# Decoder block on one core: gates of the last two attention-output jobs loaded a row block sooner, sums of the gated weights in place, another written order

## The chip, the cores and the metric

The kernel runs on one core of one Trainium2 chip. Each engine takes its instructions in order: PE (TensorE matmul, with its weight load PEld), DVE (VectorE), ACT (ScalarE), POOL (GpSimd) and SP (SyncE), which here only issues DMAs. Engines wait for each other and for DMAs through semaphores. The metric is the device time of one execution in microseconds (us); lower is better. The time before is 2249.14 us, the median of 3 runs (2249.02 to 2251.96).

## The reference

One block with a recurrent and an attention branch. What matters here is its end:

```python
y_rnn = (hr * silu(z_rnn)) @ w_out_rnn
y_attn = (o * silu(z_attn)) @ w_out_attn
merged = sigmoid(g_r + bg_r) * y_rnn + sigmoid(g_a + bg_a) * y_attn
x = x + gate[:, None, :] * (merged @ w_o)
return rms_norm(x, g_final)
```

The sequence has 2048 positions, the model 1024 channels. All is float32.

## The kernel before

**Splitting.** A float32 matmul is made of three on rounded operands: a value is split into a high part (rounded by ACT, `hi_act`, L158) and a low part (value less high, by DVE, `lo_dve` L167, or by POOL, `lo_pool` L164). `mm3` (L152) then adds high times high, high times low and low times high. All matmuls are therefore recorded at L150.

**Output jobs.** `steps` (L1657) computes both branch outputs, transposed, in eight jobs: four column blocks of 512 positions for the recurrent branch, then four for attention. A job has eight row blocks of 128 channels, so there are 64 row blocks, numbered 0 to 63 here (`t` in the code). A row block is eight steps k, each one `mm3` of a 128 x 128 weight and a y tile of 128 x 512. The first six jobs (blocks 0 to 47) are spread between the units of attention; the last two (blocks 48 to 63, columns 1024 to 2047) run on their own, 128 steps one after another, with only the work of the next stage beside them. The change is in these.

**Weights.** The weights of a row block come in two pieces of four steps, so 128 pieces in all; piece x lies in tile S0 to S3, by x % 4. `load_w` issues piece x + 3 in the second step of piece x on SP's queue, and SP waits there until PE has done with the tile. From piece 98 on the weight comes raw (L1673, from `wR`, 256 KB) and is split on the core: `split_w`, high on ACT, low on DVE, recorded at L158 and L167 as S<-S.

**Gates.** The sum of a row block (pj in PSUM) is multiplied by the attention gate and the gated recurrent output is added: `load_g` loads the two gate tiles fg (L1712, from `gaT` and `mrT`) in step 3 of the block, `evict` (L1717 the product, L1719 the add, both DVE) runs in step 1 of the next block, and `store` (L1724, SP) writes the block to `meT` in step 7 of the next. The four fg buffers hold two row blocks; which buffer a tile gets is the tile framework's choice, and a load waits for the last reader or for the store of what lay in it.

**The y tiles.** The eight y tiles of the next job are loaded (L346, four buffers R) and split while the last rows of a job run; in this stage ACT makes the highs, POOL the lows of even k and DVE those of odd k.

**Rows of the next stage.** Beside these steps `w_o` is made ready for the last stage, a seven-product scheme on 2 x 2 blocks (`product`, `output_pair`). For each of four row pairs k, `load_rows` loads two rows blocks of `w_o` (128 x 1024 each, st1/st2 or st3/st4), `gate_rows` multiplies them by the residual gate (L1849, POOL), `difference` makes four sums T1 to T4 (L1861, DVE), and `high` and `low` split the three blocks and four sums that the scheme needs. `build_rows` gives each of these a step: 10, 34, 74 and 98 for the four row pairs, and an offset. An offset fixes only the place in each engine's order; an engine does an instruction as soon as it is at its head and its operands are there. All these tables are written by hand.

**Queues.** SP's order mixes weight pieces, gates, stores and y tiles, and a load that waits for its buffer holds all behind it. A DMA on SP also waits for the one eight issues earlier.

After block 63 the stage of `output_pair` starts (lines 1958 to 2056), with PE at work without waits worth naming until about 2225 us.

Of the kernel before, what the change touches and what calls it, by code (L numbers as in the profile page):

```python
# [10 lines left out]
F32 = mybir.dt.float32  # L11
# [4 lines left out]
ALU = mybir.AluOpType  # L16
# [4 lines left out]
P = 128  # L21
S = 2048
D = 1024
KT = D // P
NB = 4
# [64 lines left out]
def decoder_block(ctx, tc, x, c, positions, g_norm, w_mod, b_mod, w_in, b_gate, conv_w, conv_b,  # L90
# [4 lines left out]
    def T(pool, shape, dt, tag, **kw):  # L95
        cnt[0] += 1
        return pool.tile(shape, dt, tag=tag, name=f"{tag}_{cnt[0]}", **kw)
# [68 lines left out]
    def lo_dve(o, i, h):  # L166
        return nc.vector.tensor_tensor(o, i, h.bitcast(F32), ALU.subtract).ins  # L167
# [1483 lines left out]
            at(e + 2, TAIL, self.store)  # L1651

    stored = set()
    RAW = 2 * KT * (NB + 2) + 1


    def steps(jobs):  # L1657
# [17 lines left out]
        def split_w(x):  # L1675
            if RAW < x < 2 * len(tiles):
                raw = W[x][:, 1].bitcast(F32)
                hi_act(W[x][:, 0], raw)
                lo_dve(W[x][:, 1], raw, W[x][:, 0])

        def load_y(j, k):
            if j < len(jobs):
# [22 lines left out]
        def load_g(t):  # L1705
            j, m = tiles[t]
            w, ys, n = jobs[j]
            at_ = slice(m * P, (m + 1) * P), slice(n * CH, (n + 1) * CH)
            G[t] = []
            for src in (grT,) if ys is yaT else (gaT, mrT):  # L1710
                g = T(fl, [P, CH], F32, "fg", bufs=4)
                nc.sync.dma_start(g[:], src[at_])  # L1712
                G[t].append(g)

# [6 lines left out]
        def store(t):  # L1721
            j, m = tiles[t]
            w, ys, n = jobs[j]
            nc.sync.dma_start((mrT if ys is yaT else meT)[m * P : (m + 1) * P, n * CH : (n + 1) * CH], G.pop(t)[0][:])  # L1724

        for k in range(KT):
            split_y(0, k)
        yield
        last = None
        for t, (j, m) in enumerate(tiles):  # L1730
            ps = T(pj, [P, CH], F32, "pj")
            for k in range(KT):
# [4 lines left out]
                    load_w(2 * t + k // KH + 3)  # L1737
                if k == 1 and t:
                    evict(t - 1, last)
                if k == 3:  # L1740
                    load_g(t)
                if k == 7 and t:
                    store(t - 1)
                wt = W[2 * t + k // KH]
                yh, yl = Y[j, k]
                mm3(ps[:], wt[:, 0, k % KH, :], wt[:, 1, k % KH, :], yh[:], yl[:], first=k == 0, last=k == KT - 1)
# [86 lines left out]
    def on(n, fn, *args):  # L1833
        pend.setdefault(n, []).append((fn, args))
# [14 lines left out]
        nc.gpsimd.tensor_tensor(v[k, i][:], v[k, i][:], v["gate"][:], ALU.mult)  # L1849

    def part(name, k):
        name = {"T3": "B12", "T4": "B21"}.get(name, name)
        if name[0] == "T":
            if (name, k) not in v:
                v[name, k] = T(fp, [P, KH, P], F32, {"T1": "s1", "T2": "s2"}[name])
            return v[name, k][:].rearrange("p k j -> p (k j)")
        i, j = int(name[1]) - 1, int(name[2]) - 1
        return v[k, i][:, j * CH : (j + 1) * CH]

    def difference(name, k, a, b):  # L1860
        tt(part(name, k), part(a, k), part(b, k), ALU.subtract)  # L1861

    def high(name, k):
        hi_act(B[name][0][:, k, :], part(name, k))
# [2 lines left out]
        lo(B[name][1][:, k, :], part(name, k), B[name][0][:, k, :])  # L1867

    def build_rows(s, k):
        on(s, gate_rows, k, 0)  # L1870
        on(s + 5, gate_rows, k, 1)
        on(s + 6, high, "B11", k)
        on(s + 7, difference, "T1", k, "B12", "B11")
        on(s + 8, low, "B11", k, lo_dve)
        on(s + 11, high, "B21", k)
        on(s + 11, difference, "T2", k, "B22", "T1")
        on(s + 12, high, "B22", k)
        on(s + 12, difference, "T3", k, "B22", "B12")
        on(s + 13, high, "T1", k)
        on(s + 13, low, "B21", k, lo_dve)  # L1880
        on(s + 15, difference, "T4", k, "B21", "T2")
        on(s + 14, low, "B22", k, lo_pool)
        on(s + 15, high, "T2", k)
        on(s + 16, high, "T3", k)
        on(s + 16, low, "T2", k, lo_dve)
        on(s + 17, high, "T4", k)
        on(s + 17, low, "T1", k, lo_pool)
        on(s + 18, low, "T4", k, lo_dve)
        on(s + 19, low, "T3", k, lo_pool)

    A, ops = {}, {}
    NP = 2 * NB
# [237 lines left out]
```

## Time and profile before

| | before |
|---|---|
| median of 3 runs | 2249.14 us |
| profiled execution, its time | 2252.27 us |
| its span, first to last instruction | 2250.5 us |
| mean granted TensorE clock | 0.985 |
| start of block 48, end of block 63 (from the order of the records) | about 1965.1 and 2087.3 us |
| PE busy and mean granted clock between these | 103.25 of 122.20 us, 0.89 |
| DVE, ACT, POOL busy between these | 94.11, 40.14, 48.75 us |

The profiled execution is one execution under the hardware profiler; its span is 1.8 us shorter than its time. In a list of instructions a row gives start, duration, engine, line, operation, out<-in, count, and in brackets how long the engine stood idle before it and what released it. PE's busy time counts modelled ends of pipelined matmuls, so a busy PE is not PE at its peak. The granted clock is a share of full speed.

### The profile page before, as it was taken

What the parts mean: (1) busy time and instruction counts of PE and PEld (TensorE: products, weight loads), DVE (VectorE), ACT (ScalarE), POOL (GpSimd) and SP (SyncE); (2) the same over time, 40 slices, a digit from 0 to 9 for tenths busy, and PEclk for the clock granted to TensorE, in tenths of its full rate; (3) what the DMA queues carried; (4) which work ended last, traced back from release to release, by engine and by line L of the source; (5) the groups of instructions that cost most, each with busy time, mean ns of one, the idle gap of its engine ahead of it and who ended that gap; (6) DMA issues with size and microseconds to landing.
All of it is one profiled execution on the core that took longest, in us unless ns stands there. A gap on an engine that the chain in (4) does not pass through costs nothing.

```text
span 2250.5 us, 34124 instructions
## 1 busy us (share of the span) xinstructions
PE 2183.3 (97%) x11326; PEld 1843.5 (82%) x11326; DVE 1442.4 (64%) x2482; ACT 1282.9 (57%) x2554; POOL 1060.3 (47%) x784
## 2 busy tenths in 40 slices
PE   8999999999999999999999999999999998988998
PEld 5998888888778988888888877888888887866786
DVE  5839887878455715445445442666667776578887
ACT  6638678767534527556456203676778877533333
POOL 2557777667556322222222102555556655334443
PEclk9999999999999999999999999999999999998999
DMA  8467887887998368888989989888988887877543
GB/s 284 117 210 262 280 301 269 295 280 261 334 282 276 111 227 277 274 299 287 299 298 304 358 285 286 272 267 255 276 263 257 250 240 227 259 248 232 180 164 113
DMA packets 412133, 577.34 MB, mean 257 GB/s; under 512 B 72406, under 2 KB 270258, under 8 KB 410932
## 3 DMA queue, kind: packets, MB, share of 16 engines
q1 hardware_dynamic: 369748, 446.75, 63.4%
q10 hardware_dynamic: 42016, 128.36, 14.9%
q8 instruction: 90, 1.47, 0.3%
q14 instruction: 87, 0.71, 0.1%
q0 software_dynamic: 192, 0.05, 0.0%
HBM read 356.92 MB, written 218.11 MB: 256 GB/s over the span
## 4 chain that ended last, share of the span: by engine, by line
PE 52%; DMA 7%; DVE 4%; issue 4%; ACT 3%; POOL 3%; SPq 1%; ACTq 0%; POOLq 0%; DVEq 0%
PE X L150 10%; PE pj L150 10%; PE V L150 9%; PE W L150 5%; PE Z L150 5%; PE Y L150 4%; PE sc L150 4%; PE o L150 3%; DMA R<-in_w_in_dram 1%; PE pg L150 1%; PE pT L1505 1%; PE pT L1518 1%; DMA vraw<-vN 1%; DMA kraw<-qT 1%; DMA kraw<-kT 1%
## 5 line engine op out<-in xcount | busy, mean ns | idle before, releaser
L150 PE MATMUL pj<-yh,S 128*128 128x512 f32 x1024 | 376.4, 413 | 21.7 <-ACT S L158 9.0
L164 POOL TENSOR_TENSOR S<-R,S 128x512 fp32r<-128x512 f32 x168 | 255.6, 1529 | 173.6 <-ACT S L158 63.8
L150 PE MATMUL V<-T,S 128*128 128x512 f32 x1344 | 326.2, 392 | 4.8 <-DVE t L454 4.6
L150 PE MATMUL X<-T,S 128*128 128x512 f32 x1344 | 324.0, 390 | 1.4 <-POOL S L164 1.0
L150 PEld LDWEIGHTS V<-T,S 128*128 128x128 f32 x1344 | 252.9, 189 | 60.0 <-DVE t L454 3.0
L150 PEld LDWEIGHTS X<-T,S 128*128 128x128 f32 x1344 | 251.5, 188 | 55.5 <-POOL S L164 1.5
L150 PEld LDWEIGHTS pj<-yh,S 128*128 128x128 f32 x1024 | 197.9, 194 | 65.7 <-ACT S L158 11.5
L150 PE MATMUL pj<-yl,S 128*128 128x512 f32 x512 | 206.9, 404 | 10.3 <-POOL yl L164 5.6
L164 POOL TENSOR_TENSOR S<-s,S 128x512 fp32r<-128x512 f32 x92 | 140.2, 1524 | 116.3 <-ACT S L158 68.3
L1421 ACT ACTIVATE pp<-pp,st 128x256 f32<-128x256 f32 (+3 forms) x256 | 133.8, 524 | 96.5 <-DVE st L1420 95.4
L150 PE MATMUL Z<-T,S 128*128 128x512 f32 x672 | 161.9, 390 | 0.0
L150 PE MATMUL Y<-T,S 128*128 128x512 f32 x672 | 161.8, 390 | 0.0
L150 PE MATMUL W<-T,S 128*128 128x512 f32 x672 | 161.7, 389 | 0.0
L150 PEld LDWEIGHTS W<-T,S 128*128 128x128 f32 x672 | 126.0, 188 | 27.0 <-issue 0.9
L150 PEld LDWEIGHTS Y<-T,S 128*128 128x128 f32 x672 | 125.9, 188 | 26.0
L150 PEld LDWEIGHTS Z<-T,S 128*128 128x128 f32 x672 | 125.8, 188 | 26.1
L167 DVE TENSOR_TENSOR ptl<-pT,pth 128x384 fp32r<-128x384 f32 (+1 forms) x160 | 97.9, 629 | 75.8 <-ACT pth L158 73.6
L164 POOL TENSOR_TENSOR s<-R,s 128x512 fp32r<-128x512 f32 x32 | 45.4, 1418 | 201.6 <-ACT s L158 178.5
L912 DVE SCALAR_TENSOR_TENSOR xc<-xr,par,xc 128x512 f32<-128x512 f32 x96 | 98.9, 1030 | 47.3 <-ACT xc L906 45.0
L158 ACT ACTIVATE S<-R 128x512 fp32r<-128x512 f32 x168 | 101.5, 622 | 47.9 <-DMA R<-in_w_in_dram 23.1
L150 PEld LDWEIGHTS pj<-yl,S 128*128 128x128 f32 x512 | 99.7, 195 | 29.4 <-POOL yl L164 7.7
L1485 ACT ACTIVATE pp<-pp,M 128x256 f32<-128x256 f32 (+3 forms) x256 | 117.9, 522 | 9.9 <-DVE M L1608 9.9
(400 smaller groups left out, 4868.8 us busy)
## 6 DMA issues: line engine op xcount, KB each, us to landing
sD<-S ACTq DMA_DIRECT2D x196, 512.0 KB, 4.1
S<-sD SPq DMA_DIRECT2D x196, 512.0 KB, 5.0
S<-wD SPq DMA_DIRECT2D x98, 512.0 KB, 5.3
R<-in_w_in_dram SPq DMA_DIRECT2D x136, 256.0 KB, 4.3
wD<-s ACTq DMA_DIRECT2D x64, 256.0 KB, 5.2
T<-in_w_mod_dram SPq DMA_DIRECT2D x8, 1024.0 KB, 11.7
vN<-ev SPq DMA_DIRECT2D x64, 128.0 KB, 2.7
zaT<-ev SPq DMA_DIRECT2D x32, 256.0 KB, 4.4
```

The source lines that it names most:

```text
L150: nc.tensor.matmul(o, lhsT=l, rhs=r, start=st, stop=sp, **kw)
L158: nc.scalar.activation(o, i, AF.Copy)
L164: nc.gpsimd.tensor_tensor(o, i, h.bitcast(F32), ALU.subtract)
L167: return nc.vector.tensor_tensor(o, i, h.bitcast(F32), ALU.subtract).ins
L912: nc.vector.scalar_tensor_tensor(xc, xr[:, i : i + CH], cw(i), xc, ALU.mult, ALU.add)
L1421: nc.scalar.activation(pdst, pdst, AF.Exp, bias=m_, scale=-1.0, accum_out=l_)
L1485: nc.scalar.activation(pp, pp, AF.Copy, scale=w)
L1505: nc.tensor.transpose(pt[:, c0 + j * P : c0 + (j + 1) * P], pp[i][:, k * P : (k + 1) * P], ident)
L1518: nc.tensor.transpose(pt[:, c * P : (c + 1) * P], pp[:, half * P : (half + 1) * P], ident)
```

## The change

In the last two jobs (`t >= TAIL0`, 48):

- the gates of a block are loaded in step 3 of the block before (block 48 in its own step 0; blocks 62 and 63 in step 0 of themselves), and every third block (2, 5, 8, 11 of the stage) takes the tiles s1 and s2 of the next stage instead of fg, so that three blocks of gates fit;
- a block is stored in step 4 of the next one, not in step 7;
- the low of every fourth weight piece (x % 4 == 0, from piece 100) is made by POOL, not by DVE;
- the four sums are formed in the gated rows themselves: T3 = B22 - B12 over B12, T2 = B11 + T3 over B11, T4 = B21 - T2 over B21, T1 = B22 - T2 over B22 (the same values; before, T1 and T2 had the tiles s1 and s2), and the offsets in `build_rows` are new, with T1 last.

```diff
--- before.py
+++ after.py
@@ -1651,7 +1651,8 @@
             at(e + 2, TAIL, self.store)
 
     stored = set()
-    RAW = 2 * KT * (NB + 2) + 1
+    TAIL0 = KT * (NB + 2)
+    RAW = 2 * TAIL0 + 1
 
 
     def steps(jobs):
@@ -1676,7 +1677,7 @@
             if RAW < x < 2 * len(tiles):
                 raw = W[x][:, 1].bitcast(F32)
                 hi_act(W[x][:, 0], raw)
-                lo_dve(W[x][:, 1], raw, W[x][:, 0])
+                (lo_pool if x % 4 == 0 else lo_dve)(W[x][:, 1], raw, W[x][:, 0])
 
         def load_y(j, k):
             if j < len(jobs):
@@ -1708,7 +1709,10 @@
             at_ = slice(m * P, (m + 1) * P), slice(n * CH, (n + 1) * CH)
             G[t] = []
             for src in (grT,) if ys is yaT else (gaT, mrT):
-                g = T(fl, [P, CH], F32, "fg", bufs=4)
+                if t >= TAIL0 and (t - TAIL0) % 3 == 2 and t < TAIL0 + 13:
+                    g = T(fp, [P, CH], F32, ("s1", "s2")[len(G[t])])
+                else:
+                    g = T(fl, [P, CH], F32, "fg", bufs=4)
                 nc.sync.dma_start(g[:], src[at_])
                 G[t].append(g)
 
@@ -1723,6 +1727,9 @@
             w, ys, n = jobs[j]
             nc.sync.dma_start((mrT if ys is yaT else meT)[m * P : (m + 1) * P, n * CH : (n + 1) * CH], G.pop(t)[0][:])
 
+        g_loads = {(0, 0): [0], (14, 0): [14], (15, 0): [15]}
+        for x in range(13):
+            g_loads[x, 3] = [x + 1]
         for k in range(KT):
             split_y(0, k)
         yield
@@ -1737,10 +1744,16 @@
                     load_w(2 * t + k // KH + 3)
                 if k == 1 and t:
                     evict(t - 1, last)
-                if k == 3:
-                    load_g(t)
-                if k == 7 and t:
-                    store(t - 1)
+                if t < TAIL0:
+                    if k == 3:
+                        load_g(t)
+                    if k == 7 and t:
+                        store(t - 1)
+                else:
+                    if k == 4:
+                        store(t - 1)
+                    for x in g_loads.pop((t - TAIL0, k), ()):
+                        load_g(TAIL0 + x)
                 wt = W[2 * t + k // KH]
                 yh, yl = Y[j, k]
                 mm3(ps[:], wt[:, 0, k % KH, :], wt[:, 1, k % KH, :], yh[:], yl[:], first=k == 0, last=k == KT - 1)
@@ -1849,16 +1862,12 @@
         nc.gpsimd.tensor_tensor(v[k, i][:], v[k, i][:], v["gate"][:], ALU.mult)
 
     def part(name, k):
-        name = {"T3": "B12", "T4": "B21"}.get(name, name)
-        if name[0] == "T":
-            if (name, k) not in v:
-                v[name, k] = T(fp, [P, KH, P], F32, {"T1": "s1", "T2": "s2"}[name])
-            return v[name, k][:].rearrange("p k j -> p (k j)")
+        name = {"T1": "B22", "T2": "B11", "T3": "B12", "T4": "B21"}.get(name, name)
         i, j = int(name[1]) - 1, int(name[2]) - 1
         return v[k, i][:, j * CH : (j + 1) * CH]
 
-    def difference(name, k, a, b):
-        tt(part(name, k), part(a, k), part(b, k), ALU.subtract)
+    def combine(name, k, a, b, op):
+        tt(part(name, k), part(a, k), part(b, k), op)
 
     def high(name, k):
         hi_act(B[name][0][:, k, :], part(name, k))
@@ -1867,26 +1876,15 @@
         lo(B[name][1][:, k, :], part(name, k), B[name][0][:, k, :])
 
     def build_rows(s, k):
-        on(s, gate_rows, k, 0)
-        on(s + 5, gate_rows, k, 1)
-        on(s + 6, high, "B11", k)
-        on(s + 7, difference, "T1", k, "B12", "B11")
-        on(s + 8, low, "B11", k, lo_dve)
-        on(s + 11, high, "B21", k)
-        on(s + 11, difference, "T2", k, "B22", "T1")
-        on(s + 12, high, "B22", k)
-        on(s + 12, difference, "T3", k, "B22", "B12")
-        on(s + 13, high, "T1", k)
-        on(s + 13, low, "B21", k, lo_dve)
-        on(s + 15, difference, "T4", k, "B21", "T2")
-        on(s + 14, low, "B22", k, lo_pool)
-        on(s + 15, high, "T2", k)
-        on(s + 16, high, "T3", k)
-        on(s + 16, low, "T2", k, lo_dve)
-        on(s + 17, high, "T4", k)
-        on(s + 17, low, "T1", k, lo_pool)
-        on(s + 18, low, "T4", k, lo_dve)
-        on(s + 19, low, "T3", k, lo_pool)
+        sub, add = ALU.subtract, ALU.add
+        for d, fn, *args in (
+            (0, gate_rows, k, 0), (4, gate_rows, k, 1), (5, high, "B11", k), (6, low, "B11", k, lo_dve),
+            (9, combine, "T3", k, "B22", "B12", sub), (9, combine, "T2", k, "B11", "T3", add),
+            (9, high, "B22", k), (9, high, "B21", k), (10, low, "B22", k, lo_pool), (10, low, "B21", k, lo_dve),
+            (11, high, "T3", k), (11, high, "T2", k), (12, combine, "T4", k, "B21", "T2", sub), (12, low, "T3", k, lo_pool),
+            (13, low, "T2", k, lo_dve), (13, high, "T4", k), (14, combine, "T1", k, "B22", "T2", sub),
+            (15, high, "T1", k), (15, low, "T4", k, lo_dve), (16, low, "T1", k, lo_pool)):
+            on(s + d, fn, *args)
 
     A, ops = {}, {}
     NP = 2 * NB
```

Three places of the order. **SP, around the start of block 48** (st are rows of `w_o` just ahead of these; S3, S0, S1 are the weight pieces 99, 100 and 101; `fg_3840`, `fg_3841` and then `fg_3849`, `fg_3850` are the gates of blocks 48 and 49; in brackets the semaphores that a DMA waits for). Before:

```order
L1673 DMA S3_3837_20539<-wR 128x512 [waits DMAHW2_49,PE_49]
L1712 DMA fg_3840_20553<-gaT 128x512 [waits DMAHW3_49]
L1712 DMA fg_3841_20555<-mrT 128x512 [waits DMAHW4_49,DVE_49]
L1673 DMA S0_3846_20573<-wR 128x512 [waits DMAHW5_49,PE_49]
L1724 DMA meT<-fg_3808_20464 128x512 [waits DMAHW6_49]
L1673 DMA S1_3848_20591<-wR 128x512 [waits DMAHW7_49,PE_49]
L1712 DMA fg_3849_20602<-gaT 128x512 [waits DMAHW0_49]
L1712 DMA fg_3850_20604<-mrT 128x512 [waits DMAHW4_49,DMAHW1_49,DVE_49]
```

After (here the gates of 48 and 49 are `fg_3837`, `fg_3838` and `fg_3842`, `fg_3843`, and S3, S0, S1 again pieces 99, 100, 101):

```order
L1716 DMA fg_3837_20536<-gaT 128x512 [waits DMAHW2_49]
L1716 DMA fg_3838_20538<-mrT 128x512 [waits DMAHW4_49,DMAHW3_49,DVE_49]
L1674 DMA S3_3839_20543<-wR 128x512 [waits PE_49]
L1716 DMA fg_3842_20557<-gaT 128x512 [waits DMAHW6_49,DMAHW5_49]
L1716 DMA fg_3843_20559<-mrT 128x512 [waits DMAHW3_49,DVE_49]
L1728 DMA meT<-fg_3808_20464 128x512 [waits DMAHW7_49]
L1674 DMA S0_3848_20578<-wR 128x512 [waits DMAHW0_49,PE_49]
L1674 DMA S1_3850_20595<-wR 128x512 [waits DMAHW1_49,PE_49]
```

Piece 99 now stands behind both gates of block 48, pieces 100 and 101 behind both gates of block 49 and a store. The DVE waits of the two mrT loads are, by the semaphores' counts, the adds (L1719, L1723 after) of block 47 and of block 48, in both programs: the buffer is the same one.

**POOL, row pairs 0 and 1** (st1 to st4 are the rows that it gates, S0 the pieces 100, 104 and 108, yl a y low). Before:

```order
L1849 TENSOR_TENSOR st1_3834_20531<-st1_3834_20531,st0_3833_20529 128x1024
L1849 TENSOR_TENSOR st2_3835_20533<-st2_3835_20533,st0_3833_20529 128x1024
L164 TENSOR_TENSOR B22l_3832_20526<-st2_3835_20533,B22h_3831_20525 128x512
L164 TENSOR_TENSOR T1l_3826_20520<-s1_3856_20645,T1h_3825_20519 128x512
L164 TENSOR_TENSOR T3l_3824_20518<-st1_3834_20531,T3h_3823_20517 128x512
L1849 TENSOR_TENSOR st3_3853_20634<-st3_3853_20634,st0_3833_20529 128x1024
L1849 TENSOR_TENSOR st4_3854_20636<-st4_3854_20636,st0_3833_20529 128x1024
L164 TENSOR_TENSOR B22l_3832_20526<-st4_3854_20636,B22h_3831_20525 128x512
```

After:

```order
L1862 TENSOR_TENSOR st1_3834_20531<-st1_3834_20531,st0_3833_20529 128x1024
L164 TENSOR_TENSOR S0_3848_20578<-S0_3848_20578 128x512
L1862 TENSOR_TENSOR st2_3835_20533<-st2_3835_20533,st0_3833_20529 128x1024
L164 TENSOR_TENSOR B22l_3832_20526<-st2_3835_20533,B22h_3831_20525 128x512
L164 TENSOR_TENSOR T3l_3824_20518<-st1_3834_20531,T3h_3823_20517 128x512
L164 TENSOR_TENSOR T1l_3826_20520<-st2_3835_20533,T1h_3825_20519 128x512
L164 TENSOR_TENSOR S0_3860_20672<-S0_3860_20672 128x512
L1862 TENSOR_TENSOR st3_3855_20639<-st3_3855_20639,st0_3833_20529 128x1024
L1862 TENSOR_TENSOR st4_3856_20641<-st4_3856_20641,st0_3833_20529 128x1024
L164 TENSOR_TENSOR S0_3870_20763<-S0_3870_20763 128x512
L164 TENSOR_TENSOR B22l_3832_20526<-st4_3856_20641,B22h_3831_20525 128x512
```

Between the two gatings of row pair 0 stands the low of piece 100; those of row pair 1 come behind T1's low (T1 is now the last sum) and behind the low of piece 104.

**DVE, the sums of row pair 0** (fg and s1 are gates, S the weight pieces). Before, from the add of block 49:

```order
L1719 TENSOR_TENSOR fg_3849_20602<-fg_3849_20602,fg_3850_20604 128x512
L1861 TENSOR_TENSOR s1_3856_20645<-st1_3834_20531 128x512
L167 TENSOR_TENSOR B11l_3820_20514<-st1_3834_20531,B11h_3819_20513 128x512
L167 TENSOR_TENSOR S2_3851_20614<-S2_3851_20614 128x512
L1861 TENSOR_TENSOR s2_3860_20669<-st2_3835_20533,s1_3856_20645 128x512
L1861 TENSOR_TENSOR st1_3834_20531<-st2_3835_20533,st1_3834_20531 128x512
L167 TENSOR_TENSOR B21l_3828_20522<-st2_3835_20533,B21h_3827_20521 128x512
L167 TENSOR_TENSOR S3_3855_20638<-S3_3855_20638 128x512
L1717 TENSOR_TENSOR fg_3857_20651<-pj_3852_20627,fg_3857_20651 128x512
L1719 TENSOR_TENSOR fg_3857_20651<-fg_3857_20651,fg_3858_20653 128x512
L1861 TENSOR_TENSOR st2_3835_20533<-st2_3835_20533,s2_3860_20669 128x512
```

After:

```order
L1723 TENSOR_TENSOR fg_3842_20557<-fg_3842_20557,fg_3843_20559 128x512
L1870 TENSOR_TENSOR st1_3834_20531<-st2_3835_20533,st1_3834_20531 128x512
L1870 TENSOR_TENSOR st1_3834_20531<-st1_3834_20531 128x512
L167 TENSOR_TENSOR S2_3853_20619<-S2_3853_20619 128x512
L167 TENSOR_TENSOR B21l_3828_20522<-st2_3835_20533,B21h_3827_20521 128x512
L1870 TENSOR_TENSOR st2_3835_20533<-st2_3835_20533,st1_3834_20531 128x512
L167 TENSOR_TENSOR T2l_3822_20516<-st1_3834_20531,T2h_3821_20515 128x512
L167 TENSOR_TENSOR S3_3857_20643<-S3_3857_20643 128x512
L1870 TENSOR_TENSOR st2_3835_20533<-st2_3835_20533,st1_3834_20531 128x512
L1721 TENSOR_TENSOR s1_3851_20606<-pj_3854_20632,s1_3851_20606 128x512
L1723 TENSOR_TENSOR s1_3851_20606<-s1_3851_20606,s2_3852_20608 128x512
```

All four sums now stand ahead of the evict of block 50 (pj_3854); before, T4 (the last row) stood behind it.

## The prediction

> **What bounds the kernel now.** I read the page first, to see which engine sets the end.
>
> ```profile
> span 2250.5 us, 34124 instructions
> PE 2183.3 (97%) x11326; PEld 1843.5 (82%) x11326; DVE 1442.4 (64%) x2482; ACT 1282.9 (57%) x2554; POOL 1060.3 (47%) x784
> ```
>
> PE sets it. The edit touches only row blocks 48 to 63, so the second view is busy time by stretch, cut there at the ends of blocks 50, 52, 55, 57, 59, 60 and 63.
>
> ```profile
> 1965.10:1987.20 22.10, 18.80 (x73) 14.40 (x72) 11.32 (x15) 5.16 (x10) 5.57 (x3) 0.92 0.87 302
> 1987.20:2008.30 21.10, 14.30 (x49) 10.72 (x49) 16.33 (x16) 5.73 (x11) 10.61 (x5) 0.84 0.53 157
> 2008.30:2026.40 18.10, 16.97 (x72) 12.80 (x71) 15.44 (x20) 7.99 (x14) 6.20 (x4) 1.00 0.93 303
> 2026.40:2046.50 20.10, 16.77 (x52) 11.49 (x51) 15.00 (x13) 6.74 (x12) 9.81 (x5) 0.75 0.85 256
> 2046.50:2057.40 10.90, 10.86 (x48) 8.64 (x47) 10.81 (x12) 4.18 (x7) 6.80 (x4) 1.00 0.67 202
> 2057.40:2069.90 12.50, 8.68 (x25) 6.39 (x26) 8.52 (x10) 3.34 (x6) 3.65 (x2) 0.73 0.72 235
> 2069.90:2087.30 17.40, 16.87 (x73) 13.36 (x72) 16.68 (x22) 7.00 (x12) 6.09 (x4) 1.00 0.57 171
> ```
>
> Columns: stretch, its length, busy time (and instructions) of PE, weight load, DVE, ACT and POOL, then granted clock, DMA share and GB/s. How long a block takes undisturbed stands in SP's timeline:
>
> ```profile
> 2046.55 0.32 SPq L1673 DMA_DIRECT2D S<-wR  x1
> ...
> 2052.00 0.32 SPq L1673 DMA_DIRECT2D S<-wR  x1
> ...
> 2057.43 0.32 SPq L1673 DMA_DIRECT2D S<-wR  x1
> ```
>
> These three weight loads wait only for PE to finish a block: 5.45 us a block when nothing is late. The seven stretches hold 3, 2, 3, 2, 2, 1 and 3 blocks; beyond 5.45 each they lose 5.75, 10.2, 1.75, 9.2, 0, 7.05 and 1.05: **35.0 us** of 122.2. That is all this edit can win. PE's own waits come third.
>
> ```profile
> 1977.57 0.73 PE L150 MATMUL pj<-yh,S 128*128 128x512 f32 x2 [1.91 <-DVE S L167]
> ...
> 1993.08 0.73 PE L150 MATMUL pj<-yh,S 128*128 128x512 f32 x2 [2.64 <-DVE S L167]
> ...
> 1999.81 0.80 PE L150 MATMUL pj<-yh,S 128*128 128x512 f32 x1 [4.16 <-ACT S L158]
> 2037.68 0.79 PE L150 MATMUL pj<-yl,S 128*128 128x512 f32 x1 [1.67 <-DVE yl L167]
> ...
> 2060.07 0.62 PE L150 MATMUL pj<-yh,S 128*128 128x512 f32 x1 [2.71 <-ACT S L158]
> ```
>
> PE waits for split weight pieces S, and after a cluster of waits the stretch's clock falls to 0.73 to 0.84, so a wait costs again about half of itself. Why the pieces are late:
>
> ```profile
> 1992.44 5.58 POOL L1849 TENSOR_TENSOR st<-st,st 128x1024 f32<-128x1024 f32 x2
> 1995.75 2.82 DVE L1861 TENSOR_TENSOR st<-st,s 128x512 f32<-128x512 f32 x1
> 1998.61 0.63 ACT L158 ACTIVATE T4h<-st 128x512 fp32r<-128x512 f32 x1 [8.27 <-DVE st L1861]
> 1999.14 1.13 ACT L158 ACTIVATE S<-S 128x512 fp32r<-128x512 f32 x2
> 2017.40 0.69 DVE L1861 TENSOR_TENSOR st<-st,s 128x512 f32<-128x512 f32 x1
> 2055.47 5.59 POOL L1849 TENSOR_TENSOR st<-st,st 128x1024 f32<-128x1024 f32 x2
> ```
>
> While POOL gates the next row pair (two L1849), DVE's sum for T4 takes 2.82 us instead of the 0.69 of row pair 1, where nothing is gated beside it. ACT's T4 high waits 8.27 us for it, and the weight highs queue behind. Row pairs 0 and 2 have such gating beside their sums (from 1992.44 and 2055.47) and lose 10.2 and 7.05; row pairs 1 and 3 have none and lose 0 to 1.75.
>
> **The change, part by part.** Durations:
>
> ```profile
> S<-wR SPq DMA_DIRECT2D x30, 256.0 KB, 4.4
> L1849 POOL TENSOR_TENSOR st<-st,st 128x1024 f32<-128x1024 f32 x8 | 21.4, 2700 | 6.3 <-DMA st<-in_w_o_dram 6.3
> L158 ACT ACTIVATE S<-S 128x512 fp32r<-128x512 f32 x30 | 18.4, 626 | 47.8 <-DMA S<-wR 22.3 <-PE pj L150 12.1 <-DVE fg L1719 6.4
> L167 DVE TENSOR_TENSOR S<-S 128x512 fp32r<-128x512 f32 x30 | 30.5, 1025 | 9.3 <-ACT S L158 9.3
> L164 POOL TENSOR_TENSOR yl<-R,yh 128x512 fp32r<-128x512 f32 x5 | 6.9, 1380 | 15.4 <-ACT yh L158 11.6 <-DMA S<-wR 3.8
> ```
>
> Nothing is computed less: four sums a row pair before and after, the same DMAs. What moves is seven weight lows (pieces 100, 104, ... 124) from DVE (1.03 each, 7.2 in all) to POOL (by the like lows of y, 1.38 each, 9.7 in all), and the order. A piece is loaded three half blocks (8.2 us) ahead of its use; 4.4 landing, 0.63 high and 1.03 or 1.38 low leave about 2 us.
>
> *Blocks 48 to 50 (before 5.75).* Here the new order hurts.
>
> ```profile
> 1968.26 0.69 DVE L1719 TENSOR_TENSOR fg<-fg,fg 128x512 f32<-128x512 f32 x1 [0.95 <-DMA fg<-mrT]
> 1968.98 0.32 SPq L1712 DMA_DIRECT2D fg<-mrT  x1
> 1969.40 0.38 SPq L1673 DMA_DIRECT2D S<-wR  x1
> ...
> 1971.76 0.32 SPq L1673 DMA_DIRECT2D S<-wR  x1
> 1974.91 2.61 DVE L167 TENSOR_TENSOR S<-S 128x512 fp32r<-128x512 f32 x1 [4.15 <-ACT S L158]
> 1977.44 0.68 DVE L1717 TENSOR_TENSOR fg<-pj,fg 128x512 f32<-128x512 f32 x1
> 1978.88 0.32 SPq L1712 DMA_DIRECT2D fg<-mrT  x1
> ```
>
> SP's second gate load of block 48 waits for the add of block 47 (1968.26), that of block 49 for the add of block 48 (issued 1978.88, behind the evict at 1977.44). In the change piece 99 stands behind the first, pieces 100 and 101 behind the second, where they went out at 1969.40 and 1971.76. So: piece 99 issued 1969.4, landed 1973.8, split by about 1975.2 (before 1977.5: 1974.91 + 2.61); evict and add of 48 to 1976.6; gate and a store issued, piece 100 out at 1977.4, landed 1981.8, high 1982.4, low on POOL 1983.8. Block 49 is through at about 1978, so PE waits 5 to 6 us at block 50, and then runs at the low clock for a block, 2 more. With under 1 us from block 49: loss 9 (7.5 to 11; the low end if the load lands in 3 us).
>
> *Blocks 51 and 52 (before 10.2).* The gating of row pair 1 now stands on POOL behind T1's low and piece 104's low, and so after the sums. What stays: three POOL lows beside the sums, 1.1 each to DVE; T1's low and piece 104's low in a row on POOL (2.8), about 1.5 late for block 52; the two L1849 beside an add and a weight low, most of it in DVE's idle time. 2.8 (1.5 to 4.5).
>
> *Blocks 53 to 55 (before 1.75).* As before, with one piece more on POOL and an add that comes behind the sums, while the store now stands ahead of two weight loads. 2.7 (1.5 to 4).
>
> *Blocks 56 and 57 (before 9.2).*
>
> ```profile
> 2026.35 0.32 SPq L346 DMA_DIRECT2D R<-oT  x1
> ...
> 2028.16 0.87 SPq L346 DMA_DIRECT2D R<-oT  x2
> 2034.27 5.58 POOL L1849 TENSOR_TENSOR st<-st,st 128x1024 f32<-128x1024 f32 x2
> 2034.79 2.84 DVE L167 TENSOR_TENSOR yl<-R,yh 128x512 fp32r<-128x512 f32 x1
> ```
>
> Block 56 starts at 2026.4 and needs the last three y's within 3.4 to 4.8 us; their loads come 0 to 2 us after its start, behind a gate load that waited. With the gates out earlier they should come 1 to 2 us before it. But the first L1849 still stands right behind y6's low, so y7's low meets it again (2.84, not 0.69); only the second L1849 moves behind piece 116. 7 (4 to 9.5).
>
> *Blocks 58 to 60 (before 7.05).* As blocks 51 and 52, with DVE further ahead: 2.2 (0.5 to 5). *Blocks 61 to 63 (before 1.05):* no gating follows; 1.3 (0.5 to 2.5). The in-place sums cost nothing by themselves: as many instructions, T2 now one sum after T3 rather than after T1, T1 last.
>
> Sum: 9 + 2.8 + 2.7 + 7 + 2.2 + 1.3 = 25.0 of loss instead of 35.0: **10 us won**. The profiled execution took 2252.27 (span 2250.5 and 1.8 around it), so 2242.3 for one like it; the median 2249.14 lies 3.1 below it, so **2239**.
>
> The Trainium skill, page "SBUF — State Buffer", section "Who interferes with whom", speaks against the seven moves: a DVE instruction with two SBUF inputs and a GpSimd one that reads SBUF exclude each other, and the second waits out the first. The trace agrees (2.82 and 2.84 beside L1849, 0.69 alone). If each of the seven lows blocked a DVE operation on the path for its whole 1.38, the sum would be up to 9.7 worse, about no change; I count a third of it.
>
> **The rivals.** *Forecast, 0.57:* as summed. *POOL's weight piece becomes what every second block waits for, 0.17, slower.* Place: the start of blocks 50, 52, ... 62; the low of a piece queues on POOL behind T1's low or an L1849 (2.70), and ACT's highs for the sums couple POOL to DVE. For it: block 50 already does so above. Against: the other six loads go out in time. Without these pieces my loss is about 15 (the 25 less some 7 at block 50, 1.5 at block 52 and 1.5 later), so it decides from (35 - 15) / 7 = 2.9 us a piece; with 4 us, clock included, 15 + 28 = 43, or 8 worse: 2257. *The queue only trades waits, 0.13, no change:* the store, now ahead of two weight loads, waits for adds that DVE makes late (in block 53 they stand behind three sums), so SP holds the weights as the gates did; blocks 53 to 57 lose 14 instead of 9.7, and 58 to 63 6 more: about 2249. *The edit does nearly all it can, 0.13:* T sums and y loads both clear, loss 7.5 + 1.5 + 1.5 + 3 + 1 + 0.5 = 15, 20 won: 2229. That the gates are not loaded sooner holds for blocks 48 and 49, as shown.
>
> **How the numbers follow.** The forecast's own bounds add up to 15.5 and 36.5 of loss; taken as independent, about 5 either side of 25, so 2234 to 2244. To hold 8 in 10 the range goes to 2230 and 2251, into the no-change case and near the best one. A measurement of this kernel tells 0.2% (4.5 us) from none. Faster than 2244.6: 0.13 + 0.57 = 0.70. Slower than 2253.6: 0.17. Between: 0.13.
>
> **What would show it.** After block 47, PE waits 4 to 6 us at block 50, released by POOL's or ACT's S, and SP's weight loads there go out after 1976. The two waits of 2.64 and 4.16 near 1993 and 2000 and the 2.71 near 2060 are gone or under 1.6, POOL's L1849 for row pairs 1 and 3 start after T1's low, and T4's sum takes 0.7 to 1.8. Near block 56 a wait for a DVE low of y stays. The product stage behind keeps its length. It is wrong if PE waits for POOL's S at most of blocks 52 to 62 (slower), or if block 50 does not wait, which would be 5 to 8 us better.

## The result and the profile after

No change that can be measured: 2250.34 us, the median of 11 runs, beside 2249.86 us, the median of 11 runs of the kernel before on the same chip; ratio 1.0001, 95% interval 0.9992 to 1.001. The profiled execution took 2248.86 us (span 2247.1), 3.4 us under that of before, and lies 1.5 us under its own median while that of before lay 2.4 us above its own here. So the 3.4 us between the two profiled executions are the draw of the run, not the change.

To see where the expected 10 us went, I count each block in PE's timeline: 24 matmuls a block, counted back from the first matmul of the product stage (X<-B11h). A block's loss is the distance of two starts less 5.44 us, two halves of 2.72. Blocks 48 to 63 took 122.2 us before and 120.7 us after (the prediction cut its stretches at rounded times, so its own losses before differ by up to 0.55 us):

| blocks | before | predicted | after |
|---|---|---|---|
| 48-50 | 5.8 | 9 (7.5 to 11) | 9.7 |
| 51-52 | 10.2 | 2.8 (1.5 to 4.5) | 4.5 |
| 53-55 | 2.3 | 2.7 (1.5 to 4) | 5.25 |
| 56-57 | 8.7 | 7 (4 to 9.5) | 7.25 |
| 58-60 | 7.05 | 2.2 (0.5 to 5) | 1.65 |
| 61-63 | 1.1 | 1.3 (0.5 to 2.5) | 5.35 |
| all | 35.2 | 25.0 | 33.7 |

The same stretches of the changed kernel in busy time, cut at the starts of blocks 48, 51, 53, 56, 58 and 61 and the end of 63 (columns as before: length, then busy time of PE, weight load, DVE, ACT and POOL, then granted clock, DMA share and GB/s):

```profile
1963.11:1989.15 26.04, 21.02 (x73) 15.03 (x72) 11.56 (x14) 5.53 (x10) 8.79 (x5) 0.87 0.79 274
1989.15:2004.50 15.35, 12.10 (x49) 8.70 (x48) 14.63 (x14) 5.64 (x10) 10.34 (x5) 1.00 0.65 209
2004.50:2026.08 21.58, 17.51 (x74) 13.20 (x72) 18.17 (x20) 8.69 (x15) 9.55 (x7) 1.00 0.87 260
2026.08:2044.20 18.12, 14.26 (x49) 9.21 (x48) 12.49 (x12) 7.21 (x13) 12.53 (x8) 0.91 0.89 281
2044.20:2062.17 17.97, 16.62 (x73) 13.44 (x72) 17.05 (x18) 6.61 (x12) 11.54 (x6) 1.00 0.73 222
2062.17:2083.84 21.67, 18.94 (x74) 14.34 (x72) 19.51 (x23) 8.00 (x15) 8.77 (x7) 0.92 0.56 183
```

Two things are to be seen. The stage now loses most where it starts (26.04 us for three blocks of 5.44). And behind it, outside blocks 56 and 57, DVE is busy 14.63 of 15.35, 18.17 of 21.58, 17.05 of 17.97 and 19.51 of 21.67 us, which is 95, 84, 95 and 90%.

PE's waits in the changed kernel:

```profile
1974.12 0.50 PE L150 MATMUL pj<-yh,S 128*128 128x512 f32 x1 [1.98 <-ACT S L158]
1981.62 0.64 PE L150 MATMUL pj<-yh,S 128*128 128x512 f32 x1 [2.63 <-ACT S L158]
...
1999.34 0.74 PE L150 MATMUL pj<-yh,S 128*128 128x512 f32 x2 [1.74 <-POOL S L164]
...
2020.96 0.73 PE L150 MATMUL pj<-yh,S 128*128 128x512 f32 x2 [2.27 <-DVE S L167]
...
2077.11 0.99 PE L150 MATMUL pj<-yh,S 128*128 128x512 f32 x2 [1.70 <-DVE S L167]
```

The waits of 2.64, 4.16 and 2.71 us of before are gone. In their place stand smaller ones for pieces from all three engines, and two at blocks 49 and 50 that SP explains:

```profile
1966.61 0.43 SPq L1674 DMA_DIRECT2D S<-wR  x1
1967.81 0.32 SPq L1716 DMA_DIRECT2D fg<-gaT  x1
1976.15 0.32 SPq L1716 DMA_DIRECT2D fg<-mrT  x1
1976.52 0.42 SPq L1728 DMA_DIRECT2D meT<-fg  x1
1977.04 0.89 SPq L1674 DMA_DIRECT2D S<-wR  x2
```

SP stands from 1967.81 to 1976.15 before the second gate load of block 49, which waits for the add of block 48 (L1723 at 1975.43 to 1976.1 in DVE's timeline); pieces 100 and 101 go out behind it.

### The profile page after: what moved, and what is told of

Same layout as the page of the kernel before. It is cut to its first block, busy times and chain, and to the rows that moved or that the text cites. A ratio compares the mean times of both kernels' runs of the same rounds, so it can differ in the third digit from the quotient of the medians.

```text
span 2247.1 us, 34124 instructions
## 1 busy us (share of the span) xinstructions
PE 2179.4 (97%) x11326; PEld 1837.1 (82%) x11326; DVE 1437.4 (64%) x2475; ACT 1283.2 (57%) x2554; POOL 1072.3 (48%) x791
## 5 line engine op out<-in xcount | busy, mean ns | idle before, releaser
L1485 ACT ACTIVATE pp<-pp,M 128x256 f32<-128x256 f32 (+3 forms) x256 | 118.0, 523 | 9.9 <-DVE M L1608 9.9
```

What stands on the lines that cost most here:

```text
L1485: nc.scalar.activation(pp, pp, AF.Copy, scale=w)
```

## The experiments

All medians are of 5 to 12 runs; the ratios are to the kernel before on the same chip, whose medians were 2249.6 to 2251.7. "Stage" is the length of blocks 48 to 63 in the profile, and the stretches are losses as in the table above. Both are from one profiled execution of each run, so small differences need care: in blocks 53 to 55 PE has the same waits in runs 4 and 8 (0.43, 1.03 and 2.29 us, and 0.44, 1.03 and 2.29), yet they lose 4.9 and 6.5. The mean granted clock there was 1.00 in run 4 and 0.93 in run 8, and 0.07 of 22.8 us is 1.6 us. A difference of that size in one stretch can be the clock alone.

| run | median us | ratio, 95% interval | stage | 48-50 | 51-52 | 53-55 | 56-57 | 58-60 | 61-63 |
|---|---|---|---|---|---|---|---|---|---|
| before | 2249.86 | | 122.2 | 5.8 | 10.2 | 2.3 | 8.7 | 7.05 | 1.1 |
| the change | 2250.34 | 0.9992-1.001 | 120.7 | 9.7 | 4.5 | 5.25 | 7.25 | 1.65 | 5.35 |
| 1 rows | 2247.37 | 0.9978-0.9996 | 118.0 | 5.25 | 8.7 | 2.1 | 9.35 | 4.65 | 1.0 |
| 2 POOL lows | 2243.86 | 0.9962-0.9985 | 112.0 | 2.5 | 4.0 | 3.7 | 10.1 | 1.4 | 3.3 |
| 3 rows, gates | 2249.31 | 0.9988-1.001 | 121.6 | 11.6 | 2.7 | 4.55 | 10.1 | 4.6 | 1.15 |
| 4 rows, POOL lows | 2241.08 | 0.9953-0.9979 | 112.6 | 2.4 | 5.1 | 4.9 | 6.9 | 1.8 | 4.4 |
| 5 change, store late | 2248.40 | 0.9984-1.0003 | 121.25 | 10.95 | 3.85 | 6.45 | 7.0 | 1.5 | 4.45 |
| 6 change, weights first | 2246.83 | 0.9989-1.0008 | 117.2 | 4.0 | 5.5 | 7.1 | 5.15 | 1.5 | 7.0 |
| 7 both of these | 2249.08 | 0.9985-1.0003 | 121.4 | 4.0 | 5.1 | 7.2 | 9.1 | 1.6 | 7.35 |
| 8 as 4, last y on POOL | 2240.44 | 0.9946-0.9974 | 110.8 | 2.2 | 5.5 | 6.5 | 2.0 | 3.8 | 3.8 |
| 9 other POOL lows | 2248.57 | 0.9976-0.9994 | 118.1 | 5.0 | 8.45 | 4.2 | 3.2 | 7.2 | 3.0 |
| 10 as 8, four lows | 2241.30 | 0.9933-0.9964 | 112.5 | 3.1 | 5.2 | 6.6 | 4.4 | 2.1 | 4.0 |
| 11 as 10, old rows | 2239.06 | 0.9936-0.9967 | 111.9 | 3.3 | 4.05 | 4.5 | 8.2 | 1.35 | 3.5 |
| 12 as 4, two gates early | 2246.61 | 0.9977-0.9999 | 121.8 | 11.9 | 3.4 | 6.55 | 7.05 | 1.5 | 4.3 |
| 13 as 4, DVE relieved | 2235.58 | 0.9918-0.9952 | 106.75 | 2.15 | 4.6 | 2.0 | 9.2 | 0.4 | 1.35 |

**1 to 4: the parts.** The change has three parts: the rows, the seven lows on POOL, and the gates with the stores.

Run 1 is the kernel before with the new `part`, `combine` and `build_rows` of the change's diff. Run 2 is the kernel before with the one line

```diff
-                lo_dve(W[x][:, 1], raw, W[x][:, 0])
+                (lo_pool if x % 4 == 0 else lo_dve)(W[x][:, 1], raw, W[x][:, 0])
```

Run 3 is the whole change without that line, run 4 the whole change with gates and stores as before:

```diff
-                if t >= TAIL0 and (t - TAIL0) % 3 == 2 and t < TAIL0 + 13:
-                    g = T(fp, [P, CH], F32, ("s1", "s2")[len(G[t])])
-                else:
-                    g = T(fl, [P, CH], F32, "fg", bufs=4)
+                g = T(fl, [P, CH], F32, "fg", bufs=4)
...
+                if k == 3:
+                    load_g(t)
+                if k == 7 and t:
+                    store(t - 1)
```

Run 1: 

> The kernel before with one part of the change alone: sums of the gated rows in place and in the new written order (the weight lows all on DVE, the gates loaded as before). Length of blocks 48 to 63 in the profile: 122.2 us before, 120.7 with the whole change, 87.2 if nothing is late. Theory A (the weight lows on POOL give the gain back): the second gating of a row pair still moves behind the sums, the waits of 2.64, 4.16 and 2.71 us go, blocks 48 to 50 keep their 5.75 us of loss: stage 108 to 112, time about 11 us under the kernel before. Theory B (the new order on SP's queue gives it back): the same here, 108 to 112. Theory C (the in-place sums do it themselves, since T1 written over B22 must wait for B22's low on POOL): PE waits for pieces behind T1's sum and high, stage 118 to 122, time within 3 us of the kernel before.

Run 2: 

> The kernel before with another part alone: every fourth weight piece's low (seven pieces) on POOL instead of DVE. Theory A: these lows queue behind the 5.58 us pair of gatings on POOL and block DVE's two-input sums, so the stage of 122.2 us grows to 126 to 134 and the time by 4 to 12 us. Theory B and theory C: POOL has the room, DVE gets 7 us back, stage 119 to 124, time within 3 us of before.

Run 3: 

> The changed kernel with the seven weight lows back on DVE (rows and gates changed). Theory A: blocks 51 to 55 and 61 to 63, which lose 4.7, 5.05 and 5.45 us in the changed kernel, lose 1 to 2.5 each; blocks 48 to 50 keep about 9 us; stage 110 to 114, 7 to 10 us faster than before. Theory B: only the lows' own length changes, stage 118 to 121. Theory C: as B, and T1's sum still comes behind B22's low and holds the pieces of blocks 61 to 63: stage 118 to 122.

Run 4: 

> The changed kernel with the gates loaded and the stores issued as before (rows and POOL lows changed). Theory A: blocks 48 to 50 go from 9.55 us of loss back to about 6, blocks 51 to 55 and 61 to 63 stay at 4.5 to 5.5 each: stage 116 to 119. Theory B: the gates were the loss, in 48 to 50 and later, stage 108 to 113 and the time 9 to 14 us under before. Theory C: stage 116 to 120, with the wait behind T1's sum at blocks 61 to 63 unchanged.

Theory A falls at once: the lows on POOL alone make the kernel faster (stage -10.2), and without them rows and gates win nothing (121.6). Neither of the others holds throughout: B fits run 4 (112.6) but expected 108 to 112 of run 1, which has 118.0; C fits runs 1 and 3 but expected 119 to 124 of run 2 and 116 to 120 of run 4. The rows alone win 4.2 us, the rows on top of the POOL lows none (112.6 to 112.0). The gates on top of both cost 8.1 (112.6 to 120.7), 7.3 of it in blocks 48 to 50. Why the rows alone bring little stands in DVE's and POOL's timelines of run 1, near block 52:

```profile
1994.56 5.60 DVE L167 TENSOR_TENSOR S<-S 128x512 fp32r<-128x512 f32 x2
```
```profile
1994.05 5.56 POOL L1849 TENSOR_TENSOR st<-st,st 128x1024 f32<-128x1024 f32 x2
```

The gating of row pair 1 does start behind the sums and meets none of them. It meets the next DVE work in line, the lows of two weight pieces, 2.8 us each instead of 0.69; PE waits 3.33 us, until 1997.44, for the first of them. The collision was moved, not removed. In run 2 DVE, and then POOL, at the same place:

```profile
1992.73 0.69 DVE L1861 TENSOR_TENSOR st<-st,s 128x512 f32<-128x512 f32 x1
```
```profile
1994.68 1.27 POOL L164 TENSOR_TENSOR S<-S 128x512 fp32r<-128x512 f32 x1 [4.34 <-ACT S L158]
1995.91 1.74 POOL L164 TENSOR_TENSOR T3l<-st,T3h 128x512 fp32r<-128x512 f32 x1
1997.62 5.66 POOL L1849 TENSOR_TENSOR st<-st,st 128x1024 f32<-128x1024 f32 x2
```

Piece 104's low stands on POOL ahead of T3's low and the gating, and waits 4.34 us for ACT. Without these 4.34 us and its own 1.27 the gating could have started at about 1992.0 (an estimate from the rows), just ahead of T4's sum at 1992.73; with them the sum, in its old order, is done first and takes 0.69 instead of 2.82. The low held POOL back. At the start of the stage piece 100's low does the same, here in POOL's timeline of run 4:

```profile
1969.52 2.39 POOL L1849 TENSOR_TENSOR st<-st,st 128x1024 f32<-128x1024 f32 x1 [5.61 <-DMA st<-in_w_o_dram]
1974.86 1.29 POOL L164 TENSOR_TENSOR S<-S 128x512 fp32r<-128x512 f32 x1 [2.95 <-ACT S L158]
1976.11 2.40 POOL L1849 TENSOR_TENSOR st<-st,st 128x1024 f32<-128x1024 f32 x1
```

In the pause between the two gatings DVE makes piece 99's low, in 0.69 us at 1972.16; before, where one gating followed the other, it took 2.61 and PE waited for it at block 49.

**5 to 7: which part of the gates costs.** Run 5 puts the store back to step 7:

```diff
-                    if k == 4:
+                    if k == 7:
                         store(t - 1)
```

Run 6 loads the gates of block 49 into the free s1 and s2 (which then also serve blocks 52, 55 and 58, in place of 50, 53, 56 and 59), and both blocks' gates behind piece 99; run 7 has both edits.

```diff
-                if t >= TAIL0 and (t - TAIL0) % 3 == 2 and t < TAIL0 + 13:
+                if t >= TAIL0 and (t - TAIL0) % 3 == 1 and t < TAIL0 + 13:
...
-        g_loads = {(0, 0): [0], (14, 0): [14], (15, 0): [15]}
+        g_loads = {(14, 0): [14], (15, 0): [15]}
         for x in range(13):
-            g_loads[x, 3] = [x + 1]
+            g_loads[x, 3] = [x + 1] if x else [0, 1]
```

Run 5: 

> The whole change, but the store of a block goes back from the fifth to the eighth step of the next block, so that the first of the two weight loads of a block is again ahead of it on SP. Blocks 48 to 63 took 122.0 us before, 120.5 with the whole change, 112.4 with rows and POOL lows but the old gates and stores. Theory D (a store that waits for DVE's add holds the weight loads behind it): pieces no longer go out in pairs right behind a store, blocks 51 to 55 and 61 to 63 win back 5 to 8 us together, stage 113 to 116, time 5 to 8 us under the kernel before. Theory E (the gate loads themselves, which wait for a buffer that an add frees, hold the weight loads): no more than 2 us come back, stage 118.5 to 121, time as before.

Run 6: 

> The whole change, but the gates of blocks 48 and 49 are loaded one after the other in block 48 behind piece 99, those of block 49 into buffers that are free, so that no gate load waits for an add ahead of pieces 99 to 101. Store places as in the change. Theory D: only blocks 48 to 50 gain, their loss goes from 9.5 to 5 to 6.5, stage 116 to 118. Theory E: the later blocks keep their gate waits too, but the start is the larger half: stage 115 to 117.

Run 7: 

> The whole change with both edits: gates of blocks 48 and 49 behind piece 99 without a wait, and the store at the eighth step. Theory D: both gains add, stage 108 to 112, time 9 to 13 us under the kernel before, at least level with the run that has rows and POOL lows alone. Theory E: as the run with the gates moved alone, within 1.5 us of it.

Theory D falls: with the store late the stage is no shorter than without that edit (121.25, 120.7). Moving the gates of blocks 48 and 49 does bring blocks 48 to 50 back to 4.0, in runs 6 and 7 alike. But 61 to 63 now lose 7, for the same reason at another place, in SP's timeline of run 6:

```profile
2056.29 0.32 SPq L1716 DMA_DIRECT2D fg<-gaT  x1
2061.64 0.32 SPq L1716 DMA_DIRECT2D fg<-mrT  x1
2062.01 0.43 SPq L1728 DMA_DIRECT2D meT<-fg  x1
2062.54 0.88 SPq L1674 DMA_DIRECT2D S<-wR  x2
```

The second gate load waits for an add that DVE ends at 2061.6, and two pieces go out behind it; PE then waits 2.90 us at the start of block 62. Neither run is told from before in time. Run 7 met neither theory's stage (121.4). Its profiled execution took 2253.72, 4.6 above its median, and differs from run 6 mainly in blocks 56 and 57 (9.1 and 5.15, at a granted clock of 0.75 and 0.89), so its stage says little beyond blocks 48 to 50.

**8: the last y.**

```diff
-                (lo_dve if k % 2 else lo_pool)(yl[:], t[:], yh[:])
+                (lo_dve if k % 2 and (j, k) != (len(jobs) - 1, 7) else lo_pool)(yl[:], t[:], yh[:])
```

> Rows and POOL lows with gates and stores as before, and the low of the last job's eighth y on POOL, ahead of the two gatings of row pair 2, instead of on DVE beside them. In the run without this PE waits 2.28 us for that low at block 57, since it takes 2.8 us beside the gating and not 0.69. If that overlap is the cost, the wait falls under 1 us and the stage goes from 112.4 to 109.5 to 111; if the y loads come too late anyway, or the low on POOL is later still behind the low of the y before it, the stage stays within 1 us of 112.4.

The low of y7 took 2.84 us on DVE beside the gating in run 4 and PE waited 2.28 us; now the wait is 0.72 and blocks 56 and 57 lose 2.0 instead of 6.9. The stage wins only 1.8: 58 to 60 lose 2.0 more, with waits of 1.01 and 1.74 us instead of one of 1.48, and 53 to 55, whose waits did not change, 1.6 more by the clock.

**9 to 11: which lows.**

Run 9 is run 2 with the first of these lines, run 10 is run 8 with the second, run 11 is run 10 with the rows of before.

```diff
-                (lo_pool if x % 4 == 0 else lo_dve)(W[x][:, 1], raw, W[x][:, 0])
+                (lo_pool if x % 4 == 2 else lo_dve)(W[x][:, 1], raw, W[x][:, 0])
...
+                (lo_pool if x in (100, 104, 116, 120) else lo_dve)(W[x][:, 1], raw, W[x][:, 0])
```

Run 9: 

> The kernel before with seven or eight weight lows on POOL as in the second run, but of the pieces 98, 102, 106, ... instead of 100, 104, 108, ...: DVE is relieved of as much work, while no such low now stands on POOL between T3's low and the gating of the next row pair. In the second run blocks 51 and 52 lost 4.0 us and 58 to 60 1.4 us, against 10.2 and 7.1 before. Theory H (the low held POOL back: it waits for its piece, so the gating behind it starts 5 us later and meets no sum): here T4's sum again takes 2 to 2.8 us beside the gating, blocks 51 and 52 lose 8 to 11 and 58 to 60 5 to 7, stage 118 to 123. Theory R (DVE has 7 us less to do): 3 to 5 and 1 to 3 us as in the second run, stage 111 to 114.

Run 10: 

> As the run with rows, POOL lows and the last y's low on POOL, but only the lows of pieces 100, 104, 116 and 120 stay on POOL; those of 108, 112 and 124 go back to DVE. That run lost 6.5 us in blocks 53 to 55 and 3.8 in 61 to 63; the kernels without POOL lows lose 2.1 to 2.3 and 1.0 to 1.1 there with the gates as before. If the lows on POOL, queued ahead of B22's and T3's, cost those, the two stretches lose 2 to 3.5 and 1 to 2, stage 104 to 107, time 12 to 15 us under the kernel before. If the order of the sums in place costs them, they stay at 5 to 6.5 and 3.5 to 4.5, stage 109 to 112.

Run 11: 

> The same four lows and the last y's low on POOL, without the change of the rows (sums and order as before). With all seven lows the rows made no difference to the stage (112.0 without, 112.6 with them). If that holds, stage 104 to 108, within 2 us of the run with the rows; if the new row order is worth something once the late lows are gone, this is 2 to 5 us longer.

Run 9 takes at least as many lows off DVE as run 2 and wins 4.1 us of stage, not 10.2; blocks 51 and 52 and 58 to 60 lose nearly what they lost before. So theory R falls. In fact the moves hardly relieved DVE: in the stage it is busy 93.9 us with 104 instructions before, and 92.6 with 97 in run 2, not 7 us less, since those that meet POOL take longer (beside a low on POOL 1.78 us instead of 0.69). Run 9 is no clean proof of H: T4's sum took 0.68 in it, since POOL stopped between the two gatings for piece 106 and it was the add ahead of the sum that took 2.17. In run 10 three lows fewer on POOL changed nothing in 53 to 55 and 61 to 63 (6.6 and 4.0), in run 11 the old rows not much (4.5 and 3.5; its stage of 111.9 missed the 104 to 108 expected). The lows of pieces 108, 112 and 124, which stand on POOL in or next to those blocks, are not what they lose by.

**12 and 13: the two questions left.**

Both start from run 4. Run 12:

```diff
-                if k == 3:
+                t0 = t - KT * (NB + 2)
+                if k == 3 and t0 not in (0, 1):
                     load_g(t)
+                if t0 == 0 and k in (0, 3):
+                    load_g(t + (k == 3))
```

Run 13, in `low`:

```diff
-        lo(B[name][1][:, k, :], part(name, k), B[name][0][:, k, :])
+        if lo is lo_dve:
+            hi_act(B[name][1][:, k, :], part(name, k))
+        else:
+            lo(B[name][1][:, k, :], part(name, k), B[name][0][:, k, :])
```

Run 13's kernel leaves out sixteen subtractions, so its result is incomplete; it measures only what they cost.

Run 12: 

> The run with rows and POOL lows (stage 112.6, blocks 48 to 50 lose 2.4), with one thing put back: the gates of block 48 are loaded at its first step and those of block 49 in block 48, as in the whole change; all later gates and all stores as before. Theory E (a gate load that waits for an add, ahead of pieces 99 to 101 on SP, is what the early gates cost): blocks 48 to 50 lose 9 to 11.5, stage 117.5 to 121, time within 4 us of the kernel before. Theory D' (the loss sits in the stores and later gates): 48 to 50 lose 2 to 5, stage 111 to 115, time 8 us or more under it.

Run 13: 

> The run with rows and POOL lows, but the sixteen lows of the gated rows that DVE makes (B11, B21, T2, T4 of each row pair) are replaced by a copy of the row on ACT: the subtraction is left out, DVE has 16 instructions fewer (0.69 us each alone, 11 us, up to 1.78 beside POOL), ACT 16 more of 0.63. In the run without this DVE is busy 34.5 of 37.7 us in blocks 51 to 55. Theory V (with the waits at the gatings gone DVE's queue is what the pieces wait for, so that a wait won in one block comes back in a later one): blocks 51 to 55 go from 10.1 us of loss to 3 to 6 and 61 to 63 from 4.4 to 1 to 2.5, stage 103 to 108. Theory K (each wait there is the chain of high, low and sum of its own row, whichever engine makes them): 51 to 55 stay at 8 to 10 and 61 to 63 at 3.5 to 4.5, stage 110 to 113.

Run 12 shows theory E: two early gate loads take the stage from 112.6 to 121.8, all of it in blocks 48 to 50 (2.4 to 11.9, somewhat over the 9 to 11.5 expected; the other stretches together 23.2 to 22.8). SP and PE there:

```profile
1970.31 0.38 SPq L1712 DMA_DIRECT2D fg<-gaT  x1
1978.07 0.32 SPq L1712 DMA_DIRECT2D fg<-mrT  x1
1978.48 0.38 SPq L1673 DMA_DIRECT2D S<-wR  x1
```
```profile
1984.10 0.79 PE L150 MATMUL pj<-yh,S 128*128 128x512 f32 x1 [4.76 <-ACT S L158]
```

Run 13 speaks for theory V. Blocks 51 to 55 go from 10.1 to 6.6 (3 to 6 was expected), 61 to 63 from 4.4 to 1.35, the stage to 106.75. DVE in blocks 51 to 55, first in run 4, then in run 13:

```profile
1981.54:2018.82 37.28, 29.63 (x121) 21.90 (x120) 34.45 (x35) 15.39 (x27) 22.28 (x12) 1.00 0.79 259
```
```profile
1983.17:2016.98 33.81, 29.19 (x122) 21.82 (x121) 24.52 (x27) 17.07 (x31) 19.05 (x10) 1.00 0.88 287
```

34.45 of 37.28 us, 92%, against 24.52 of 33.81, 73%. With the sixteen instructions their collisions with POOL went too, so the run shows what DVE's work costs together with these, not each apart. POOL was not relieved (busy 61.1 us of the stage in run 4, 61.6 in run 13), and in run 4 none of PE's waits in 53 to 55 and 61 to 63 ends with POOL.

Of the kernels that compute all, runs 2, 4, 8, 10 and 11 are faster than the kernel before by 0.26 to 0.51% (0.15 to 0.36% at the near ends of their intervals); the five intervals overlap, so none is told from the others.

## Why the prediction was wrong

**Blocks 48 to 50: the mechanism was right, and the size** (9 predicted, 9.7 measured). Gates before pieces 99 to 101, gate loads that wait for adds, a wait at block 50: as written. But the wait at block 50 was 2.63 us, not 5 to 6; 1.98 fell on the second half of 49, and the loss beyond the waits was 4.7 us, not the 2 put down for the clock, so that the sum came out near is partly luck. What it missed is that these blocks would otherwise have fallen to 2.4, since piece 100's low holds the second gating back. So the early gates cost 7.3 us here (with the stores) and 9.5 in run 12, and not the 3.25 between the 5.75 and 9 of the sum.

**Blocks 51, 52 and 58 to 60: the gating no longer meets T4's sum, as said, but mostly for another reason.** They lose 4.5 and 1.65 instead of 10.2 and 7.05. I credited the new order of rows; by itself it leaves 8.7 and 4.65, since the gating then meets the lows of pieces on DVE. The seven lows on POOL bring these stretches to 4.0 and 1.4 without the rows. The prediction does name piece 104's low as one of the two that the gating stands behind, but its sum counted these lows only as a cost.

**Blocks 53 to 55 and 61 to 63: the step that failed.** The terms 2.7 and 1.3 came out as 5.25 and 5.35, with 51 and 52 at the edge of their range (4.5 for 2.8): 8.3 us, four fifths of the 10 forecast. "No gating follows" was taken to mean that nothing is late there, and what the moved gating of row pair 1 meets, an add and a weight low, was put "most of it in DVE's idle time". There is no such time: DVE is busy 14.63 of 15.35 us in blocks 51 and 52, the low (piece 106's) takes 2.9 us, and PE waits for it at block 53. The sum gave every stretch the loss of its own collision and let DVE catch up for nothing; the 35.0 us over 5.45 a block were called all there is to win, and PE's pace the floor. In the kernel before, DVE used PE's long stalls to catch up. There its lows for the first pieces of blocks 53 and 61 (each the first of a pair) are done by 2003.6 and 2065.3, 4.5 and 4.35 us ahead of PE; in the changed kernel PE waits for the same two. DVE before, then PE after:

```profile
2002.93 1.28 DVE L167 TENSOR_TENSOR S<-S 128x512 fp32r<-128x512 f32 x2
2064.65 1.29 DVE L167 TENSOR_TENSOR S<-S 128x512 fp32r<-128x512 f32 x2
```
```profile
2005.51 0.73 PE L150 MATMUL pj<-yh,S 128*128 128x512 f32 x2 [0.39 <-DVE S L167]
2063.22 0.73 PE L150 MATMUL pj<-yh,S 128*128 128x512 f32 x2 [0.44 <-DVE S L167]
```

With that lead gone, whatever stands in DVE's queue is late for PE, directly or through ACT, whose highs of pieces queue behind the highs of rows that wait for DVE's sums. So in block 54 of the changed kernel, in DVE's, ACT's and PE's timelines:

```profile
2012.02 1.66 DVE L1870 TENSOR_TENSOR st<-st,st 128x512 f32<-128x512 f32 x1
2013.72 0.63 ACT L158 ACTIVATE T4h<-st 128x512 fp32r<-128x512 f32 x1 [2.76 <-DVE st L1870]
2014.26 0.61 ACT L158 ACTIVATE S<-S 128x512 fp32r<-128x512 f32 x1
2014.92 0.50 PE L150 MATMUL pj<-yh,S 128*128 128x512 f32 x1 [1.40 <-ACT S L158]
```

The share of busy time alone does not tell the two kernels apart: before, DVE was busy 16.68 of 17.40 us in blocks 61 to 63, where PE lost 1.1. Runs 10 and 11 rule out the lows of pieces 108, 112 and 124 on POOL, and run 13 shows DVE's work to be what the same stretches lose by; but run 13 started from run 4, so for the changed kernel itself the cause rests on the rows shown. At 61 to 63 the wait of 1.70 us is of this kind: ACT waits 3.46 us for T1's sum ahead of the highs of two pieces. The wait of 0.59 is of another: its piece went out at 2060.81, right behind a store on SP that waited for an add, and ACT had it only at 2067.30. What of the 5.35 goes to each was not taken apart further; run 4, with the old gates, has 4.4 there.

**Blocks 56 and 57** were right in number (7 predicted, 7.25 measured) and in part of the mechanism: y7's low meets the gating. But the last y loads did not come 1 to 2 us ahead of block 56; they went out 0.3 us before its start and 2.3 us after it, as late as before, so the near agreement is partly luck. Run 8 takes the collision away, and some 2 us of the 4.9 come back in 58 to 60, where PE then waits longer.

**The rivals.** The one in which the queue only trades waits, with no change, gave the right time by the wrong carrier: not mainly the stores (run 5), but the gate loads at the start and DVE's queue behind. The slower one, POOL's piece at every second block, fell with runs 2 and 4, though in the changed kernel PE waits four times for POOL's piece, 4.0 us in all. The rule of the Trainium skill (page "SBUF — State Buffer", section "Who interferes with whom") holds for each pair of instructions (two lows of 5.60 us beside two gatings of 5.56), but adding up blocked time piece by piece gave the wrong sign for the seven lows: one of them, placed ahead of the larger POOL instruction, kept that away from DVE.

## What to carry to other kernels

A prefetch on an in-order queue is early only if its buffer is free then; a load whose buffer is freed by the same work it should run ahead of holds everything behind it, and here two such loads cost 7.3 us in the change and 9.5 in run 12. Where two engines exclude each other, moving an instruction moves the collision to what stands next in line: ask what that is, and whether an instruction that waits can hold the big one back. And before counting a stall as winnable, add up what the second engine has to do in that stretch with its collisions: its busy time, not the first engine's pace, may be the floor.

## What was not expected of the hardware

How unevenly the exclusion is shared. A DVE low that starts while a gating runs ends some 0.55 us after it, whatever it costs: 0.69 us alone, up to 2.9 here. The gating pays only where a DVE instruction with two SBUF inputs is already under way as it starts, and then some 0.45 us (2.8 to 2.94 instead of 2.39); in run 4 the gating at 1976.11 kept its 2.40 while the low that started 0.03 us behind it took 2.91. The product that reads PSUM (L1717) stayed at 0.68 us and ACT's copies at 0.61 to 0.64 throughout. Nor was it expected that many short waits cost PE no less than few long ones: 20.1 us of waits in the changed kernel, none over 2.63, go with 33.7 us of loss, and 18.9 us before, up to 4.16, with 35.2; the granted clock of blocks 48 to 50 fell to 0.87. In the changed kernel's trace the clock is 0.50 for 3.41 us at a time, four times in the stage (from 1975.00, 1981.82, 2033.02 and 2077.40); in the 3.41 us ahead of each PE was busy 1.43, 0.78, 1.73 and 1.72 us, and none of the waits there was longer than 2.63 us. So a wait does not cost a fixed share of itself: in blocks 51 to 55, at a granted clock of 1.00, 7.3 us of waits go with 9.7 of loss, and in 61 to 63, with one such drop, 2.7 with 5.35.
